# The first slab of a rotary-embedding kernel loaded by eight DMAs of every eighth partition

## The chip, the cores and the metric

The kernel runs on one core of a Trainium2 chip. The metric is the device time in microseconds (us), the median of repeated runs. Engines have the profile's names: ACT is the scalar engine, DVE the vector engine, SP the engine whose queue issues the loads.

## The reference

The input `x` is float32 of shape 16 x 512 x 1024 (batch, sequence, dimension), and the dimension is 16 heads of 64. Each head is rotated with a `cos` and a `sin` of its sequence position. The output is float32 of the same size.

```python
x = x.reshape(batch, seq, num_heads, head_dim)
x1, x2 = x[..., :half_dim], x[..., half_dim:]
rotated = np.concatenate([x1 * cos - x2 * sin, x1 * sin + x2 * cos], axis=-1)
```

So 33.55 MB come in and 33.55 MB go out, whatever the kernel does.

## The kernel before

The work is cut into 8 slabs of 2 batches each, 4 MB per slab. A slab lies in SBUF (the core's working memory of 128 partitions) as 128 rows of W = 8192 float32, 32 KB in each partition. One DMA loads it and one stores it. Five slab buffers are in turn; the first five loads are issued at once.

```python
    def dram(t, s, a=0, n=W):
        return bass.AP(tensor=t.tensor, offset=t.offset + s * nb * seq * dim + a,
                       ap=[[W, P], [1, n]])
    # ...
    def load(s):
        slab[s] = slabs.tile([P, W], f32, tag="slab", name="slab")
        nc.sync.dma_start(out=slab[s], in_=dram(x, s))

    load(0)
    # ... cos and sin are loaded with two small DMAs ...
    for s in range(1, slots):          # slots = 5
        load(s)
```

For each slab ACT casts to bf16, DVE multiplies twice and adds, ACT casts back to float32, and ACT's queue issues the store; then the slab's buffer is loaded again.

```python
        nc.scalar.copy(out=xs, in_=xu)
        if r + n == rpp:
            nc.scalar.dma_start(out=dram(out_flat, s), in_=slab[s])
            if s + slots < nslabs:
                load(s + slots)
```

Of the kernel before, what the change touches and what calls it, by code (L numbers as in the profile page):

```python
# [2 lines left out]

# [4 lines left out]


@with_exitstack  # L10
def kernel(
    ctx: ExitStack,
    tc: tile.TileContext,
    x: bass.AP,
    cos: bass.AP,
    sin: bass.AP,
    num_heads: int,
    out: bass.AP,
):
    nc = tc.nc  # L20
    P = nc.NUM_PARTITIONS

    batch, seq, dim = x.shape
    nh = num_heads
    hd = dim // nh
    half = hd // 2
    bf16 = mybir.dt.bfloat16
    f32 = mybir.dt.float32

    nb = 2  # L30
    slots = 5
    nslabs = batch // nb
    rpp = nb * seq // P
    W = rpp * dim
    SP = seq // rpp
    TW = rpp * half

    out_flat = out.rearrange("b s h d -> b s (h d)")

    singles = ctx.enter_context(tc.tile_pool(name="singles", bufs=1))  # L40
    slabs = ctx.enter_context(tc.tile_pool(name="slabs", bufs=slots))
    xpool = ctx.enter_context(tc.tile_pool(name="xpool", bufs=2))
    psum = ctx.enter_context(tc.tile_pool(
        name="psum", bufs=1, space=bass.MemoryType.PSUM))
# [7 lines that stand above are left out]
    def view(t, offset, *dims):  # L52
        return dataclasses.replace(t, offset=t.offset + offset,
                                   ap=[t.ap[0], *[list(d) for d in dims]])


    slab = {}


    def load(s):  # L60
        slab[s] = slabs.tile([P, W], f32, tag="slab", name="slab")
        nc.sync.dma_start(out=slab[s], in_=dram(x, s))  # L62


    load(0)


    TR = seq // P
    G = rpp // TR
    raw = singles.tile([P, 2 * TR * half], f32, tag="raw")  # L70
    for i, src in enumerate((cos, sin)):
        nc.gpsimd.dma_start(out=view(raw, i * TR * half, (1, TR * half)), in_=bass.AP(  # L72
            tensor=src.tensor, offset=src.offset,
            ap=[[TR * half, P], [1, TR * half]]))

    for s in range(1, slots):
        load(s)


    pick = singles.tile([P, G * P], bf16, tag="pick")  # L80
    nc.gpsimd.memset(pick, 0.0)  # L81
    for g in range(G):
        part = view(pick, g * P, (SP, P // SP), (1, SP))
        nc.gpsimd.affine_select(  # L84
            out=part, in_=part, compare_op=mybir.AluOpType.not_equal, fill=1.0,
            base=-g, pattern=[[0, P // SP], [-G, SP]], channel_multiplier=1)

    tab1 = singles.tile([P, 2 * TR * half], bf16, tag="tab1")
    nc.vector.tensor_copy(out=tab1, in_=raw)  # L89
    acc = psum.tile([P, 2 * TW], f32, tag="acc")  # L90
    for i in range(2):
        for g in range(G):
            nc.tensor.matmul(view(acc, i * TW + g * TR * half, (1, TR * half)),  # L93
                             view(pick, g * P, (1, P)),
                             view(tab1, i * TR * half, (1, TR * half)),
                             start=True, stop=True)

    tab = singles.tile([P, 2 * rpp * hd], bf16, tag="tab")
    nc.vector.tensor_copy(out=view(tab, 0, (hd, 2 * rpp), (1, half)),  # L99
                          in_=view(acc, 0, (half, 2 * rpp), (1, half)))  # L100
    nc.vector.tensor_copy(out=view(tab, half, (hd, rpp), (1, half)),  # L101
                          in_=view(acc, 0, (half, rpp), (1, half)))
    nc.vector.tensor_scalar_mul(  # L103
        out=view(tab, rpp * hd + half, (hd, rpp), (1, half)),
        in0=view(acc, TW, (half, rpp), (1, half)), scalar1=-1.0)

    xb = {}


    def cast(u):  # L110
        s, r, n = u
        if r == 0:
            xb[s] = xpool.tile([P, W], bf16, tag="xb", name="xb")
        nc.scalar.copy(out=view(xb[s], r * dim, (1, n * dim)),  # L114
                       in_=view(slab[s], r * dim, (1, n * dim)))



    passes = []
    for s in range(nslabs):  # L120
        n = rpp if s < nslabs - 2 else rpp // 2
        passes += [(s, r, n) for r in range(0, rpp, n)]


    cast(passes[0])
    for i, (s, r, n) in enumerate(passes):
        if i + 1 < len(passes):
            cast(passes[i + 1])
        xs = view(slab[s], r * dim, (1, n * dim))
        xu = view(xb[s], r * dim, (1, n * dim))  # L130

        t2 = view(slab[s].bitcast(bf16), 2 * r * dim, (1, n * dim))
        for t, a in ((t2, rpp * hd), (xu, 0)):
            nc.vector.tensor_mul(  # L134
                out=t, in0=xu,
                in1=view(tab, a + r * hd, (hd, n), (0, nh), (1, hd)))
        nc.vector.tensor_add(  # L137
            out=xu, in0=xu, in1=view(t2, half, (hd, n * nh), (-half, 2), (1, half)))
# [8 lines that stand above are left out]
# [1 line left out]
_INS = ['x', 'cos', 'sin', 'num_heads']  # L148
_OUTS = [((16, 512, 16, 64), 'float32')]

_NUMBERS = {'num_heads': 16}


# [26 lines left out]
```

## Time and profile before

| | before |
|---|---|
| time, median of 4 runs | 162.27 us (161.70 to 163.23) |
| span of the profiled run (that run took 163.08 us) | 161.3 us |
| DVE busy, ACT busy | 67%, 70% |
| DMA engine time: loads (q1), stores (q10) | 49.1%, 48.2% |
| first slab issued, landed | 0.74 us, 13.32 us |

The 16 DMA engines work 97.3% of the span, so this is a kernel bound by its transfers.

### The profile page before, as it was taken

The numbers are of one execution on the slowest core, as the hardware profiler recorded it, in microseconds if no ns is written. First come the engines' busy times: TensorE is split into PE (matmuls) and PEld (weight loads), VectorE is DVE, ScalarE is ACT, GpSimd is POOL, SyncE is SP. The second block draws the span as 40 slices with busy tenths as digits, with TensorE's granted clock in tenths as the row PEclk, the third lists the DMA queues.
The fourth block names the chain that finished last, engine by engine and source line by source line (L and its number), as shares of the span: only waits on it lengthen the run. The fifth ranks groups of instructions, "written<-read, shape, count | busy, mean of one in ns | idle before, by whom it ended". The sixth has DMA issues, their size and how long they took to land.

```text
span 161.3 us, 153 instructions
## 1 busy us (share of the span) xinstructions
PE 0.6 (0%) x4; PEld 0.4 (0%) x4; DVE 108.7 (67%) x34; ACT 113.5 (70%) x21; POOL 2.3 (1%) x9
## 2 busy tenths in 40 slices
PE   0010000000000000000000000000000000000000
PEld 0000000000000000000000000000000000000000
DVE  0012099999969997998899499939739399940000
ACT  3006939469899899989987997089994999653000
POOL 5000000000000000000000000000000000000000
DMA  7999999999989999999999999999999999999992
GB/s 260 406 406 390 520 390 390 520 390 390 488 349 463 390 439 471 390 439 471 382 447 455 398 447 455 398 447 455 390 439 463 398 431 471 398 431 471 398 431 106
DMA packets 2368, 67.24 MB, mean 417 GB/s; under 512 B 288, under 2 KB 288, under 8 KB 320
## 3 DMA queue, kind: packets, MB, share of 16 engines
q1 hardware_dynamic: 1152, 33.55, 49.1%
q10 hardware_dynamic: 1152, 33.55, 48.2%
q0 software_dynamic: 64, 0.13, 0.2%
HBM read 33.69 MB, written 33.55 MB: 417 GB/s over the span
## 4 chain that ended last, share of the span: by engine, by line
DMA 42%; ACT 33%; DVE 13%; issue 2%; ACTq 0%; SPq 0%
DMA slab<-in_x_dram 25%; DMA out_dram<-slab 18%; ACT slab L140 17%; ACT xb L114 16%; DVE slab L134 4%; DVE xb L134 4%; DVE xb L137 4%; ACTq L142 0%; ACTq L140 0%; SPq L62 0%
## 5 line engine op out<-in xcount | busy, mean ns | idle before, releaser
L114 ACT CAST xb<-slab 128x8192 bf16<-128x8192 f32 (+1 forms) x10 | 56.5, 5652 | 25.2 <-DMA slab<-in_x_dram 24.0
L140 ACT CAST slab<-xb 128x8192 f32<-128x8192 bf16 (+1 forms) x10 | 56.5, 5650 | 7.2 <-DVE xb L137 7.2
L134 DVE TENSOR_TENSOR slab<-xb,tab 128x8192 bf16<-128x8192 bf16 (+1 forms) x10 | 35.7, 3572 | 21.9 <-ACT xb L114 21.8
L137 DVE TENSOR_TENSOR xb<-xb,slab 128x8192 bf16<-128x8192 bf16 (+1 forms) x10 | 35.7, 3572 | 0.3
L134 DVE TENSOR_TENSOR xb<-xb,tab 128x8192 bf16<-128x8192 bf16 (+1 forms) x10 | 35.7, 3572 | 0.3
L89 DVE CAST tab<-raw 128x256 bf16<-128x256 f32 x1 | 0.3, 294 | 11.0 <-DMA raw<-in_sin_dram 11.0
L114 ACT ACT_TABLE_LOAD x1 | 1.3, 1283 | 0.7 <-PEq L161 0.7
L99 DVE CAST tab<-acc 128x512 bf16<-128x512 f32 x1 | 0.7, 691 | 0.7 <-PE acc L93 0.7
L72 POOL DMA_DIRECT2D raw<-in_cos_dram x1 | 0.7, 674 | 0.8 <-POOLq L161 0.8
L93 PE MATMUL acc<-tab,pick 128*128 128x128 bf16 x4 | 0.6, 302 | 11.3 <-DVE tab L89 11.3
L84 POOL TENSOR_SCALAR_AFFINE_SELECT pick<-pick 128x128 bf16<-128x128 bf16 x2 | 0.5, 288 | 0.1
L72 POOL DMA_DIRECT2D raw<-in_sin_dram x1 | 0.5, 534 | 0.0
L93 PEld LDWEIGHTS <-pick 128*128 128x128 bf16 x4 | 0.4, 127 | 11.2 <-issue 8.0
L101 DVE CAST tab<-acc 128x256 bf16<-128x256 f32 x1 | 0.4, 415 | 0.0
L103 DVE TENSOR_SCALAR tab<-acc 128x256 bf16<-128x256 f32 x1 | 0.4, 415 | 0.0
L81 POOL MEMSET pick<- 128x256 bf16 x1 | 0.3, 330 | 0.0
L161 POOL MEMSET const-float32-0.0<- 128x1 f32 x1 | 0.1, 99 | 0.2 <-issue 0.2
L161 POOL MEMSET const-bfloat16-1.0<- 128x1 bf16 x1 | 0.1, 102 | 0.0
L161 POOL MEMSET const-uint8-127<- 128x1 uint8 x1 | 0.1, 102 | 0.0
L161 POOL MEMSET const-float32-1.0<- 128x1 f32 x1 | 0.1, 99 | 0.0
## 6 DMA issues: line engine op xcount, KB each, us to landing
slab<-in_x_dram SPq DMA_DIRECT2D x8, 4096.0 KB, 27.3
out_dram<-slab ACTq DMA_DIRECT2D x8, 4096.0 KB, 24.0
raw<-in_cos_dram POOLq DMA_DIRECT2D x1, 64.0 KB, 7.0
raw<-in_sin_dram POOLq DMA_DIRECT2D x1, 64.0 KB, 9.0
```

What stands on the lines that cost most here:

```text
L72: nc.gpsimd.dma_start(out=view(raw, i * TR * half, (1, TR * half)), in_=bass.AP(tensor=src.tensor, offset=src.offset, ap=[[TR * half, P], ...
L81: nc.gpsimd.memset(pick, 0.0)
L84: nc.gpsimd.affine_select(out=part, in_=part, compare_op=mybir.AluOpType.not_equal, fill=1.0, base=-g, pattern=[[0, P // SP], [-G, SP]], c ...
L93: nc.tensor.matmul(view(acc, i * TW + g * TR * half, (1, TR * half)), view(pick, g * P, (1, P)), view(tab1, i * TR * half, (1, TR * half)) ...
L99: nc.vector.tensor_copy(out=view(tab, 0, (hd, 2 * rpp), (1, half)), in_=view(acc, 0, (half, 2 * rpp), (1, half)))
L101: nc.vector.tensor_copy(out=view(tab, half, (hd, rpp), (1, half)), in_=view(acc, 0, (half, rpp), (1, half)))
L103: nc.vector.tensor_scalar_mul(out=view(tab, rpp * hd + half, (hd, rpp), (1, half)), in0=view(acc, TW, (half, rpp), (1, half)), scalar1=-1.0)
L114: nc.scalar.copy(out=view(xb[s], r * dim, (1, n * dim)), in_=view(slab[s], r * dim, (1, n * dim)))
L134: nc.vector.tensor_mul(out=t, in0=xu, in1=view(tab, a + r * hd, (hd, n), (0, nh), (1, hd)))
L137: nc.vector.tensor_add(out=xu, in0=xu, in1=view(t2, half, (hd, n * nh), (-half, 2), (1, half)))
L140: nc.scalar.copy(out=xs, in_=xu)
L161: nc = _bacc.Bacc("TRN2", target_bir_lowering=False, num_devices=1)
```

## The change

Its intent is to give each of the 16 DMA engines one 32 KB row per DMA, eight times, instead of eight rows in one DMA. The bytes are the same.

```diff
-    load(0)
+    slab[0] = slabs.tile([P, W], f32, tag="slab", name="slab")
+    for p in range(P // 16):
+        nc.sync.dma_start(
+            out=slab[0][p::P // 16, :],
+            in_=bass.AP(tensor=x.tensor, offset=x.offset + p * W,
+                        ap=[[P // 16 * W, 16], [1, W]]))
```

## The prediction

The sum came to +9.0 us on 162.1 us, 171.1 us: +9.75 us for packets of the first slab that take twice the 1.22 us of the trace before, -0.4 us for sooner first bytes and another -0.3 us. The factor two and the -0.3 us stand as my estimates only. This slower case was given about 70%, with 169.5 to 173 us.

> **What bounds the kernel now.** I read the page first, its slices and its DMA queues. In the slices each digit is a fortieth of the span in tenths of busy time, and the row of GB/s is what the DMA engines moved.
>
> ```profile
> DMA  7999999999989999999999999999999999999992
> GB/s 260 406 406 390 520 390 390 520 390 390 488 349 463 390 439 471 390 439 471 382 447 455 398 447 455 398 447 455 390 439 463 398 431 471 398 431 471 398 431 106
> ...
> q1 hardware_dynamic: 1152, 33.55, 49.1%
> q10 hardware_dynamic: 1152, 33.55, 48.2%
> ...
> HBM read 33.69 MB, written 33.55 MB: 417 GB/s over the span
> ```
>
> The DMA row has a 9 (or one 8) from the second slice to the last but one: the 16 DMA engines are never out of work. Loads (q1) take 49.1% and stores (q10) 48.2% of all engine time, 97.3% together. No compute engine comes near: the page has DVE at 67% and ACT at 70%. From q1 I also get the unit that I need: 0.491 x 161.3 us x 16 engines = 1267 us for 8 loads x 128 rows of 32 KB = 1024 data packets, so 1.24 us for one 32 KB packet; q10 gives 1.22 us. That is 32,768 B / 1.22 us = 26.9 GB/s for one engine. A load of 4 MB is 8 such packets on each engine, 9.7 to 9.9 us.
>
> Next the chain that ended last, for its beginning and its longest pieces, and the list of waits.
>
> ```profile
> 0.74 12.58 DMA slab<-in_x_dram
> 13.32 0.02 issue
> 13.34 7.03 ACT xb L114
> ...
> 69.62 28.29 DMA out_dram<-slab
> 97.90 0.02 SPq L62
> 97.93 0.03 issue
> 97.96 27.38 DMA slab<-in_x_dram
> ```
> ```profile
> ACT xb L114 <- DMA slab<-in_x_dram: 24.0, 5, 11.3
> ```
>
> The chain starts with the very load that is changed: issued at 0.74 us, landed at 13.32 us. Of these 12.58 us some 9.8 are the packets and 2.8 are start and landing. ACT sits idle 11.3 us for it, and the first cast waits for the whole slab, not for pieces. The middle pieces look like compute and transfers in turn, but the slices say that the DMA engines are full through all of it, so the time is set by when they start, at which rate they run, and how long the tail is after them. Last the issuing queue and the end of the span:
>
> ```profile
> L62 SPq DMA_DIRECT2D slab<-in_x_dram x8: 328/398/600, 0.7 to 98.0; - x8
> ```
> ```profile
> 0.74 2.49 SPq L62 DMA_DIRECT2D slab<-in_x_dram  x5
> ```
> ```profile
> 150.00:155.00 5.00, 0.00 (x0) 0.00 (x0) 0.00 (x0) 0.00 (x0) 0.00 (x0) 1.00 1.03 446
> 155.00:158.00 3.00, 0.00 (x0) 0.00 (x0) 0.00 (x0) 0.00 (x0) 0.00 (x0) 1.00 0.96 415
> 158.00:161.30 3.30, 0.00 (x0) 0.00 (x0) 0.00 (x0) 0.00 (x0) 0.00 (x0) 1.00 0.07 30
> ```
>
> The first is the load's line (min/median/max ns of an issue), the second the timeline: all five first loads are issued in 2.49 us, without waits between them. The third is the busy table by stretch, whose last two columns are DMA share and GB/s: the engines run at full rate until about 158 us, then there is the landing of the last store.
>
> [...]
>
> **The change part by part.**
>
> *Bytes and packets: nothing.* 8 DMAs x 16 rows are the same 128 packets of 32 KB, 8 per engine[...]. The other 15 transfers of 4 MB stay.
>
> *Issues: added, but hidden.* SP gets 8 issues in place of 1. At the 0.33 to 0.60 us of the load's line they cost 2.6 to 4.8 us at the very most, and a DMA of 16 rows should be no dearer to issue than one of 128. An engine has 1.22 us or more of work from each, so it isn't starved; loads 1 to 4 are issued some 3 us later, when the engines are still busy with slab 0. Cost 0. The first issue now makes 16 rows instead of 128, so the first bytes may flow a little sooner: I take -0.4 us, a guess bounded by the 2.8 us of start and landing.
>
> *[...] this is where I expect the cost.* DMA number p writes partitions p, p+8, ... p+120[...] a packet takes 2 x 1.22 = 2.44 us and the slab 8 x 2.44 = 19.5 us in place of 9.75: +9.75 us. [...] I take -0.3 us. Compute is no part of it.
>
> *Who pays.* [...] no store exists yet (the first is issued at 40.88 us), so nothing fills the half-used engines. Slab 0 lands at 13.3 + 9.0 = 22.3 us, slab 1 some 10 us later, all stores later by the same, and the engines are full from then on as before. The lost time of the bound is not made good: +9.75 - 0.4 - 0.3 = **+9.0 us**, and 162.1 + 9.0 = **171.1 us**.
>
> *Waits.* [...] Some 0.1 us, in the rounding.
>
> **The rivals.**
>
> A. *The engines bind[...].* Then each engine has the same 8 packets at 1.22 us and nothing else changes; the earlier first byte gives up to 0.5 us: 161.6 to 162.3 us, the same. [...]
>
> B. *The eight DMAs wait for each other*, because their targets lie interleaved in one buffer, or because semaphores are used again. Each would cost start and landing, 2.8 + 1.2 = 4.0 us, eight of them 32 us in place of 12.6: +19 us, 181 us. Against it: the rows are disjoint, and the timeline has no wait between the loads of before. A milder form, in which only loads 1 to 4 wait for single pieces, costs nothing, as these are issued long before their turn.
>
> C. [...] the loss is smaller, 3 to 7 us, 165 to 169 us. [...]
>
> D. *The loss is hidden later.* It would need idle DMA time to be eaten up. The slices have none between the second and the last but one, so I give this next to nothing.
>
> **Range and chances.** [...] C another 8%, B 4%, and A 18%. A lies within 2% (158.9 to 165.3 us), nearly all the rest above. Faster by 2% would need over 3 us; the whole start and landing of slab 0 is 2.8 us, so almost nothing. Range 165.5 to 173.5 us, which leaves out A and B. Chances: faster 0.01, same 0.19, slower 0.80.
>
> **What would show it.** If right: the first piece of the chain grows from 12.58 to some 21.6 us; ACT's longest wait for the load from 11.3 to about 20; in a table by stretch the GB/s from 4 to 20 us lie near 215 while the DMA share stays near 1 (packets are longer, not fewer); the share of q1 stays near 49% or rises, as 128 packets cost 1.22 us more each (156 us of engine time: 1267 + 156 = 1423 us over 16 x 170.3 us is 52%); from 25 us on, the slices look as before, and the tail is the same. Wrong: if the stretch from 4 to 12 us shows some 420 GB/s, A holds; if it has gaps in the DMA share with waits of SP between issues of the first slab, B; if GB/s begin low and climb within the slab, C. If slab 0 lands late but the end doesn't move, D.

## The result

The changed kernel takes 172.06 us (171.81 to 172.16, 4 runs) against 162.27 us: slower, with a ratio of 1.0595 (95% interval 1.0541 to 1.0648). A ratio here is the mean time of one kernel's runs over that of the other's in the same rounds, so it isn't quite the ratio of the medians quoted beside it.

The page of the changed kernel, first its slices and the load queue:

```profile
DMA  5989979999999999999999898989898989898985
GB/s 133 268 185 193 239 285 455 409 455 409 455 409 455 409 455 432 432 439 424 463 401 478 385 486 378 486 378 486 378 486 378 486 378 486 378 493 378 486 378 239
...
q1 hardware_dynamic: 1264, 33.56, 52.0%
```

The DMA row is as full as before, but for the first six slices, some 25 us, the engines move only 133 to 285 GB/s. They are as busy as before and work at about half the speed. The load queue takes 52.0% of 16 x 170.0 us, 1414 us, where before it took 1267 us for the same bytes.

The busy table by stretch says it more exactly. Its columns are PE, PE weight load, DVE, ACT and POOL busy us, the clock, then DMA share and GB/s. A packet counts in the stretch in which it starts, so a share can be a little over 1. Before:

```profile
4.00:12.00 8.00, 0.59 (x4) 0.32 (x3) 0.35 (x2) 0.00 (x0) 0.00 (x0) 1.00 0.97 418
12.00:20.00 8.00, 0.00 (x0) 0.00 (x0) 1.30 (x3) 6.66 (x1) 0.00 (x0) 1.00 1.01 434
20.00:28.00 8.00, 0.00 (x0) 0.00 (x0) 7.57 (x2) 5.31 (x2) 0.00 (x0) 1.00 0.97 418
...
15.00:155.00 140.00, 0.00 (x0) 0.00 (x0) 107.06 (x30) 110.52 (x20) 0.00 (x0) 1.00 1.01 431
```

and after, each with a long stretch of its steady part added:

```profile
4.00:12.00 8.00, 0.58 (x4) 0.31 (x3) 1.65 (x4) 0.00 (x0) 0.00 (x0) 1.00 1.04 217
12.00:20.00 8.00, 0.00 (x0) 0.00 (x0) 0.00 (x0) 0.00 (x0) 0.00 (x0) 1.00 1.00 209
20.00:28.00 8.00, 0.00 (x0) 0.00 (x0) 0.00 (x0) 4.03 (x2) 0.00 (x0) 1.00 0.99 348
...
26.00:162.00 136.00, 0.00 (x0) 0.00 (x0) 107.06 (x30) 111.43 (x20) 0.00 (x0) 1.00 1.00 432
```

From 4 to 20 us the rate is 217 and 209 GB/s where it was 418 and 434. From 26 us on it is 432 GB/s, the old rate (431). Nothing is lost after the first slab, and nothing is won back.

The chain that ended last (followed back from the last instruction, each step to what released it), at its beginning, after:

```profile
0.74 0.57 SPq L68
...
5.23 18.64 DMA slab<-in_x_dram
...
23.96 1.28 ACT L120
```

The slab lands at 5.23 + 18.64 = 23.87 us, 10.55 us later than before. Two smaller things are new. The issue of one of the eight DMAs takes 0.57 us. And ACT loads its activation table (L120, 1.28 us) after the slab has landed; before, that was done at 0.74 us, while ACT waited. ACT now has four semaphore instructions at this line, from 16.6 to 23.9 us, and the table load stands behind those waits. Last come the wait of ACT and the waits of the issuing queue (total us, times, longest us), and the issues of the changed line (min/median/max ns):

```profile
ACT L120 <- DMA slab<-in_x_dram: 24.0, 1, 24.0
```
```profile
SPq L62 <- DMA slab<-in_x_dram: 14.4, 5, 4.8
```
```profile
L68 SPq DMA_DIRECT2D slab<-in_x_dram x8: 567/589/681, 0.7 to 5.2; - x8
```

The second shows that loads 1 to 4 now wait for landed pieces of slab 0 before they are issued: by the timeline they go out from 6.12 to 16.90 us, where before all five loads were out by 3.23 us. They still come in time: the DMA share is 1.04, 1.00 and 0.99 in the three stretches from 4 to 28 us.

For single packets I read the DMA packet records of the traces. The first number is the start of the first 32 KB packet of slab 0, in us from the start of the run's own span; then come the median durations (us) of its first 16 packets by start (taken as one per engine; the records kept don't name the engine), the next 16, and so on to the eighth. All kernels of this table but the first are explained in this document's experiments.

```
                          start   1st  2nd  3rd  4th  5th  6th  7th  8th
before                     1.76  1.93 1.22 1.21 1.21 1.21 1.22 1.22 1.21
after                      2.08  2.39 2.47 2.44 2.55 2.33 2.55 2.55 2.55
e2 sixteen neighbours      1.77  3.91 4.53 4.58 4.35 4.53 4.54 4.55 4.56
e4 every fourth            2.07  1.87 1.24 1.21 1.21 1.21 1.21 1.21 1.21
e5 halves in turn          2.09  2.25 2.39 2.23 2.31 2.31 2.31 2.31 2.31
e6 staggered, first trial  2.28  2.03 1.77 1.81 1.66 1.58 1.52 1.50 1.50
e9 staggered, second       2.11  2.25 1.67 1.55 1.40 1.46 1.34 1.42 1.42
e11 32 neighbours          1.78  2.29 2.56 2.55 2.54 2.51 2.58 2.55 2.56
```

(In e6 and e9 the eight packets of the added DMA shift the groups a little.) In the changed kernel a packet takes 2.55 us once the start is over, slightly more than twice 1.21 us.

### The profile page after: what moved, and what is told of

Same layout as the page of the kernel before. It is cut to its first block, busy times and chain, and to the rows that moved or that the text cites. A ratio compares the mean times of both kernels' runs of the same rounds, so it can differ in the third digit from the quotient of the medians.

```text
span 170.0 us, 169 instructions
## 1 busy us (share of the span) xinstructions
PE 0.6 (0%) x4; PEld 0.4 (0%) x4; DVE 108.7 (64%) x34; ACT 113.5 (67%) x21; POOL 2.3 (1%) x9
## 3 DMA queue, kind: packets, MB, share of 16 engines
q1 hardware_dynamic: 1264, 33.56, 52.0%
q10 hardware_dynamic: 1152, 33.55, 45.7%
HBM read 33.69 MB, written 33.55 MB: 395 GB/s over the span
## 4 chain that ended last, share of the span: by engine, by line
DMA 42%; ACT 33%; DVE 12%; SPq 2%; issue 2%; ACTq 0%
DMA slab<-in_x_dram 27%; ACT slab L146 17%; ACT xb L120 15%; DMA out_dram<-slab 15%; DVE xb L143 4%; DVE slab L140 4%; DVE xb L140 4%; SPq L68 2%; ACT L120 1%; ACTq L148 0%; ACTq L120 0%; ACTq L146 0%; SPq L62 0%
## 5 line engine op out<-in xcount | busy, mean ns | idle before, releaser
L120 ACT CAST xb<-slab 128x8192 bf16<-128x8192 f32 (+1 forms) x10 | 56.5, 5652 | 10.0 <-DMA slab<-in_x_dram 8.7
```

The costliest lines, as they stand in the source:

```text
L120: nc.scalar.copy(out=view(xb[s], r * dim, (1, n * dim)), in_=view(slab[s], r * dim, (1, n * dim)))
```

## The experiments

The theory to test is that the cost comes from which partitions are written at the same moment: in the change, 16 that lie eight apart. Why some sets of partitions should be slower than others is not shown by any run, and the mechanism that I had assumed is cut. The rivals to tell apart are the splitting itself (eight small DMAs, their issues and waits), DRAM rows 256 KB apart, and "a DMA's rate follows from the partitions that it writes as a whole" against "what counts is which partitions are written at the same moment". Every experiment was timed in 3 rounds beside the kernel before; the medians of that were 162.28 to 162.88 us.

| run | slab 0 (unless said) | time, us | ratio, 95% interval |
|---|---|---|---|
| e1 | 8 DMAs, 128 partitions, an eighth of the columns | 162.04 | 0.9959 (0.992 to 0.9997) |
| e2 | 8 DMAs of 16 neighbours | 188.38 | 1.158 (1.1537 to 1.1623) |
| e3 | as the change, DRAM rows in a row | 171.52 | 1.0549 (1.0502 to 1.0596) |
| e4 | 4 DMAs of every fourth partition | 162.94 | 1.0034 (0.9984 to 1.0085) |
| e5 | 8 DMAs, halves in turn | 170.45 | 1.0508 (1.0469 to 1.0548) |
| e6 | e5 and one 8-row DMA ahead | 168.61 | 1.0401 (1.0347 to 1.0454) |
| e7 | the last store split, load as before | 171.08 | 1.0558 (1.0487 to 1.063) |
| e8 | the change, table load early | 172.03 | 1.061 (1.0572 to 1.0648) |
| e9b | e5, upper half first | 170.84 | 1.0508 (1.0449 to 1.0566) |
| e9 | e9b and one 8-row DMA second | 166.19 | 1.0229 (1.0165 to 1.0292) |
| e10 | load 6 split, slab 0 as before | 174.62 | 1.0733 (1.0662 to 1.0803) |
| e11 | 4 DMAs of 32 neighbours | 171.99 | 1.0581 (1.0529 to 1.0633) |

The diffs below are shortened. Those of e1 to e5, e9b and e11 are against the change (with `P // 16` written as 8), that of e6 and e9 against its control, that of e8 against the change, those of e7 and e10 against the kernel before.

### e1: eight DMAs over all partitions

```diff
+    C = W // 8
     for p in range(8):
-        nc.sync.dma_start(out=slab[0][p::8, :], in_=...)
+        nc.sync.dma_start(out=view(slab[0], p * C, (1, C)), in_=dram(x, 0, p * C, C))
```

> Eight DMAs for the first slab, but each of all 128 partitions and an eighth of the columns (4 KB per row). [...] packets run at the full rate and the slab lands at about 13.5 to 14.5 us; time 162 to 164 us. Rival, the splitting into eight small DMAs costs the time by itself (their issues, their start and landing, their semaphores): landing near 24 us and about 172 us.

The line by stretch of e1:

```profile
4.00:12.00 8.00, 0.58 (x4) 0.31 (x3) 1.65 (x4) 0.00 (x0) 0.00 (x0) 1.00 1.03 411
```

411 GB/s and 162.04 us: eight issues and the waits that come with them cost nothing that can be seen here. The rival of the splitting falls. The ratio is below 1 by 0.4% with an interval that nearly touches 1; I take it as the same time.

### e2: the same DMAs with 16 neighbouring partitions

```diff
-            out=slab[0][p::8, :],
-            in_=bass.AP(tensor=x.tensor, offset=x.offset + p * W,
-                        ap=[[8 * W, 16], [1, W]]))
+            out=slab[0][16 * p:16 * p + 16, :],
+            in_=bass.AP(tensor=x.tensor, offset=x.offset + 16 * p * W,
+                        ap=[[W, 16], [1, W]]))
```

> Eight DMAs of 16 neighbouring partitions each, one 32 KB row per engine as in the change; only which partitions go together differs. [...] a packet takes four times 1.22 us, the slab 39 us in place of 19.5: landing near 43 us, 190 to 193 us. Rival, what costs is one-descriptor DMAs: about 172 us as with the change. Rival, the DRAM rows 256 KB apart: these are neighbours now, so about 162 us.

```profile
20.00:28.00 8.00, 0.00 (x0) 0.00 (x0) 0.83 (x3) 0.00 (x0) 0.00 (x0) 1.00 1.04 119
```

119 GB/s with the engines fully busy, packets of 4.5 us, 188.38 us. Against the change only the choice of partitions differs, and DRAM rows that are neighbours; against e3 below, which reads these very DRAM rows and took 171.52 us, nothing but the partitions differs. With 16 neighbours the packet takes 3.7 times the 1.21 us of before, with every eighth partition (2.55 us) 2.1 times. The four times of the expectation was an estimate of mine. The time is 1.6 us under the expected band; packets of 4.5 us in place of 4 x 1.22 = 4.88 us would account for it.

### e3: DRAM rows one after the other

```diff
-            in_=bass.AP(tensor=x.tensor, offset=x.offset + p * W,
-                        ap=[[8 * W, 16], [1, W]]))
+            in_=bass.AP(tensor=x.tensor, offset=x.offset + 16 * p * W,
+                        ap=[[W, 16], [1, W]]))
```

> As the change on the SBUF side (every eighth partition), but the 16 rows of each DMA lie one after the other in DRAM. The result is wrong on purpose: slab 0's rows are permuted. [...] nothing changes against the change, 171 to 173 us. Rival, DRAM rows 256 KB apart are read slowly: 162 to 163 us.

```profile
4.00:12.00 8.00, 0.58 (x4) 0.31 (x3) 0.36 (x2) 0.00 (x0) 0.00 (x0) 1.00 1.03 216
```

216 GB/s against 217: the distance of the rows in DRAM has no part in it. Its output is wrong, which doesn't matter for the time. The time is 0.5 us under the change's.

### e4: four DMAs of every fourth partition

```diff
-    for p in range(8):
+    for p in range(4):
         nc.sync.dma_start(
-            out=slab[0][p::8, :], ...            ap=[[8 * W, 16], [1, W]]))
+            out=slab[0][p::4, :], ...            ap=[[4 * W, 32], [1, W]]))
```

The first band is for a rate set by the partitions written at one moment, the second for one set by all the partitions of a DMA.

> Four DMAs of every fourth partition, 32 rows each, two per engine. [...] If what counts is[...] written at the same moment: 169.5 to 172 us, a little under the change[...]. If what counts is[...] a DMA reaches as a whole: 162 to 163 us.

```profile
4.00:12.00 8.00, 0.59 (x4) 0.32 (x3) 1.65 (x4) 0.00 (x0) 0.00 (x0) 1.00 1.07 459
```

Full rate, packets of 1.21 us, 162.94 us. My first band rested on an assumption of how the 32 rows are dealt to the engines, which no run shows. Either only the partitions of a whole DMA count, or the rows are dealt differently from what I assumed. The next runs had to decide whether the moment counts at all.

### e5, e9b: the controls

With 16 rows to a DMA it matters less how they are dealt: in the trace of the change, which has 16 rows to a DMA too, 16 packets are under way at each whole us from 3 to 23 us. Here they are every fourth partition of one half, the lower (0 to 63) or the upper (64 to 127).

```diff
-    for p in range(8):
-        nc.sync.dma_start(out=slab[0][p::8, :], ...)
+    for p in range(4):
+        for h in (0, 64):              # e9b: (64, 0)
+            nc.sync.dma_start(
+                out=slab[0][h + p:h + 64:4, :],
+                in_=bass.AP(tensor=x.tensor, offset=x.offset + (h + p) * W,
+                            ap=[[4 * W, 16], [1, W]]))
```

> Control for the next run. Eight DMAs of 16 rows, every fourth partition of one half: 0, 4, .. 60, then 64, 68, .. 124, then 1, 5, .. 61 and so on. [...] half rate as in the change[...]: 169.5 to 171.5 us. Rival, something particular to every eighth partition: 162 to 163 us.

> Control for the next run: the halves in turn, upper half first. Same as the halves in turn before, 170 to 171 us.

170.45 and 170.84 us, as expected; the line of e5:

```profile
4.00:12.00 8.00, 0.58 (x4) 0.31 (x3) 1.65 (x4) 0.00 (x0) 0.00 (x0) 1.00 1.08 241
```

Packets take 2.31 us against 2.55; in the change the fifth packet is the short one (2.33 us). Why these are shorter is not shown.

### e6, e9: the same DMAs, with half of the engines one packet behind

A DMA of 8 rows adds 8 packets under 512 B where each of the others adds 16 (q1 of e6 has 1280 packets: 1032 rows, 15 x 16 small packets of the other DMAs and 8 of this one), which I read as 8 engines in place of 16. Put into the queue, it is meant to make these one packet late for all that follows, so that with halves in turn some engines write to the lower half while the others write to the upper; the records don't name the engines, so this isn't seen directly. The added rows go into slab 1's buffer, which load 1 overwrites later (and waits for; the lines that allocate this buffer early and load it are left out of the diff). e6 has the added DMA first, on rows of the lower half, e9 second, on rows of the upper half, which the first DMA has written to. In both expectations the first band is for a full rate by staggering, the second for a cost that the moment has no part in.

```diff
+        if i == 0:                     # e9; in e6 ahead of the loop, rows 0:32:4
+            nc.sync.dma_start(
+                out=slab[1][64:96:4, :],
+                in_=bass.AP(tensor=x.tensor, offset=x.offset, ap=[[4 * W, 8], [1, W]]))
```

> The control with one more DMA ahead of it: 8 rows of 32 KB (into slab 1's buffer, which load 1 overwrites after)[...]. [...] full rate again in spite of more bytes, 162.5 to 165 us with about 1.2 us for the added packet. [...] 1.2 us above the control, 171 to 173 us.

> The staggering tried once more, with the added 8-row DMA second in the queue[...]. In the first trial (168.6 us) packets took about 1.5 us[...]. [...] first packet 2.4 us, then 1.22 to 1.4 us each, 165 to 167 us. [...] as the control and one packet, 171.5 to 172.5 us.

e6 took 168.61 us. That is over its band of 162.5 to 165, and still 1.8 us under its control although it moves more. Its packets of 1.50 to 1.81 us were still longer than 1.21 us, for a reason not shown, and I placed the added DMA differently. e9 took 166.19 us, inside its band, 4.7 us under its control e9b, with 256 KB more to move. The stretch from 4 to 12 us of e9, then of e9b:

```profile
4.00:12.00 8.00, 0.58 (x4) 0.32 (x3) 1.65 (x4) 0.00 (x0) 0.00 (x0) 1.00 1.01 344
...
4.00:12.00 8.00, 0.06 (x1) 0.05 (x1) 0.29 (x1) 0.00 (x0) 0.00 (x0) 1.00 1.03 225
```

Packets went from 2.36 us (e9b) to 1.34 to 1.67 us. The DMAs of slab 0 are the same ones, on the same partitions; only what is under way beside what has changed. So the rate isn't a property of a single DMA: at 344 GB/s against 225, it depends on what is written at the same moment. If that had no part in it, 171.5 to 172.5 us were expected. Two ends stay open. The packets are still above 1.21 us, and why isn't known; and no run staggers engines that stay on one half of the partitions, which would tell this apart from any other good that working on two DMAs at once may do.

### e11: four DMAs of 32 neighbouring partitions

What the run can show is whether 32 neighbours are as slow as the 16 of e2 (a quarter of the rate) or run like every eighth partition (half of it).

```diff
+    for p in range(4):
+        nc.sync.dma_start(
+            out=slab[0][32 * p:32 * p + 32, :],
+            in_=bass.AP(tensor=x.tensor, offset=x.offset + 32 * p * W,
+                        ap=[[W, 32], [1, W]]))
```

> Four DMAs of 32 neighbouring partitions, two rows per engine[...]. It asks how the rows of a DMA of 32 are dealt to the engines, which decides how every fourth partition (162.9 us) is to be understood. (a) [...] a quarter of the rate, 186 to 190 us. [...] (b) [...] half the rate, 170 to 172 us. (c) Only[...] that a DMA reaches as a whole count, whatever the dealing[...], half the rate, 170 to 172 us.

```profile
12.00:20.00 8.00, 0.59 (x4) 0.32 (x3) 1.01 (x3) 0.00 (x0) 0.00 (x0) 1.00 1.07 219
```

171.99 us, half the rate (190 GB/s from 4 to 12 us): (a), a quarter of the rate, is refuted as I had put it, (b) and (c), half of it, both fit. How 32 rows are dealt to the engines, and so how e4 is to be understood, is not shown. The practical reading doesn't need it: four DMAs over every fourth partition run at full rate (459 GB/s from 4 to 12 us, e4), four over neighbours at half.

### e7: the last store instead of the first load

```diff
-            nc.scalar.dma_start(out=dram(out_flat, s), in_=slab[s])
+            if s < nslabs - 1:
+                nc.scalar.dma_start(out=dram(out_flat, s), in_=slab[s])
+            else:
+                for p in range(8):
+                    nc.scalar.dma_start(
+                        out=bass.AP(tensor=out_flat.tensor, offset=out_flat.offset
+                                    + s * nb * seq * dim + p * W,
+                                    ap=[[8 * W, 16], [1, W]]),
+                        in_=slab[s][p::8, :])
```

> The kernel before, with its last store split as the change splits the first load: eight DMAs of every eighth partition out of SBUF. [...] the last slab takes 19.5 us in place of 9.7, some of it beside the store before it, 168 to 172 us. If only writes into SBUF meet this limit: 162 to 163 us.

```profile
150.00:155.00 5.00, 0.00 (x0) 0.00 (x0) 0.00 (x0) 0.00 (x0) 0.00 (x0) 1.00 1.13 243
155.00:160.00 5.00, 0.00 (x0) 0.00 (x0) 0.00 (x0) 0.00 (x0) 0.00 (x0) 1.00 0.96 249
```

243 and 249 GB/s at the end, where the kernel before had 446 from 150 to 155 us; 171.08 us. The engines are as busy as before (shares of 1.13 and 0.96), so this read from SBUF slows down much as the load did (217 and 209 GB/s). The step between the rows in DRAM, which e3 clears for loads, wasn't tested alone for a store.

### e8: the table load taken off the chain

```diff
+    warm = singles.tile([P, 1], f32, tag="warm")
+    nc.vector.memset(warm, 0.0)
+    nc.scalar.copy(out=warm, in_=warm)
```

> The change with a copy of one element on ACT at the start, so that the 1.28 us activation table load is done before the waits and not after them (in the changed kernel it moved from 0.7 us to 24 us, onto the chain). If the DMA engines set the end: stores start 1.3 us sooner and nothing comes of it, 171.5 to 172.5 us. If the chain's compute pieces are the bound: 1.3 us less, 170.5 to 171 us.

The table load was back at 0.74 us, and the issues of the stores, min/median/max ns and first and last start, show the first one at 51.6 us, where the changed kernel has 52.8:

```profile
L152 ACTq DMA_DIRECT2D out_dram<-slab x8: 338/338/374, 51.6 to 155.3; - x8
```

The time stayed at 172.03 us. 1.2 us sooner on the chain's compute bought nothing. This is also why the pieces "ACT" and "DVE" of the chain, nearly half of it by share, must not be read as a bound here.

### e10: load 6 split, in mid-kernel

```diff
     def load(s):
         slab[s] = slabs.tile([P, W], f32, tag="slab", name="slab")
-        nc.sync.dma_start(out=slab[s], in_=dram(x, s))
+        # s == 6: eight DMAs out=slab[s][p::8, :] as in the change; else as before
```

> The kernel before with load 6, in mid-kernel beside stores, split as the change splits the first load. If the loss is the same wherever there is a full DMA queue: about 9 us, 170 to 172 us. If the stores that share the engines fill the time[...]: clearly less, 163 to 168 us.

174.62 us, worse than either reading. Three lines of its table by stretch, the two queues of its page, and the issue of its eight DMAs in the timeline (start, us from the first to the end of the last):

```profile
90.00:100.00 10.00, 0.00 (x0) 0.00 (x0) 4.34 (x2) 10.00 (x2) 0.00 (x0) 1.00 1.03 331
140.00:150.00 10.00, 0.00 (x0) 0.00 (x0) 6.32 (x3) 10.00 (x3) 0.00 (x0) 1.00 0.83 357
150.00:160.00 10.00, 0.00 (x0) 0.00 (x0) 7.44 (x4) 6.54 (x3) 0.00 (x0) 1.00 0.73 315
```
```profile
q1 hardware_dynamic: 1264, 33.56, 49.0%
q10 hardware_dynamic: 1152, 33.55, 45.8%
```
```profile
78.18 22.11 SPq L64 DMA_DIRECT2D slab<-in_x_dram  x8
```

Beside stores, and with its pieces spread over a longer time, the rate falls less, to 331 GB/s rather than 217 and 209. But the eight issues took 22.11 us, as the queue waited between them for earlier transfers (its list of waits has 23.6 us on stores and 9.3 us on loads at that line), the slab came late for the compute, and towards the end the DMA engines ran dry: shares of 0.83 (140 to 150 us) and 0.73, where no 10 us stretch of the kernel before, from 30 to 150 us, is under 0.97. So there are both longer packets and idle engines in the 11.7 us, and the queues say how much is which: packets took 94.8% of 173.3 us, 164.3 us per engine, against 97.3% of 161.3 us, 156.9 us, before. That is 7.4 us of longer packets; the remaining 4.6 us of the 12.0 us by which the span grew are time without packets. That the waits between the issues made it idle is argued, not tested. Neither expectation had the waits.

## Why the prediction was right

It forecast 171.1 us (165.5 to 173.5) and 172.06 was measured. By its steps:

- *Bytes and packets, nothing.* Right: 1264 packets on q1 are the 1152 of before and 7 x 16 packets of 4 bytes, and the megabytes are the same (33.56 against 33.55).
- *Packets twice as long, +9.75 us.* Right that the choice of partitions costs it: e1, e2, e3, e5 and e9 single it out against the splitting, DRAM and the DMAs as such. The mechanism is not shown. In size: load time on q1 went from 1267 to 1414 us, which is 147 us over 16 engines, +9.2 us, where the prediction had 9.75 - 0.3 = 9.45. The two small tables take part (q0 from 0.2% to 0.4% of engine time, +0.35 us).
- *The -0.3 us.* About right in size: one packet of eight was shorter by 0.2 us (2.33 against 2.55 us). The reason for it no run shows.
- *First bytes, -0.4 us.* Wrong in sign. The first packet started at 2.08 us in place of 1.76, +0.3 us. The first issue took 0.57 us in place of 0.37 (medians of the line 0.59 and 0.40), where I had said that 16 rows should be no dearer than 128; as 16 neighbours took 0.42 us (e2) and every eighth partition 0.59 us with the same DRAM rows (e3), it is the step between the rows in SBUF that is dear, not their number. The 2.8 us that bounded the guess were misread, too: by the packet records before, 1.0 us pass from the first issue to the first packet and 0.5 us from the last packet to the landing; the rest lies among the packets, whose first took 1.93 us.
- *Issues hidden.* Right that they don't starve the engines: the DMA share was 1.04 and 1.00 while the slab came in. But loads 1 to 4 were issued 5 to 14 us later than before, by their waits, and not some 3 us later.
- *Who pays.* Right: 432 GB/s from 26 to 162 us against 431 from 15 to 155 us before, so the loss stays. By the packet records the last one ends at 168.7 us against 160.1, which is 8.6 us, as the span grew by 8.7 us. That is less than the 9.8 us of the medians because the profiled run of before was one of its slower ones (163.08 us) and that of after its fastest (171.81): before, three last packets ended late, at 159.2, 160.0 and 160.1 us, the others by 158.9. The mean end of the last 16 packets of 4 bytes in the store queue is 168.4 us against 158.8, 9.7 us.
- *Waits, 0.1 us.* Here it overlooked that the table load goes behind the waits: 1.28 us on the chain. e8 shows that this was worth nothing in time.

The measured terms, 9.2 + 0.35 + 0.3 us, make 9.9 us, and the time grew by 9.8 us. The forecast sum was 9.05 us: the start explains some 0.7 of the 0.8 us that it lacked. A little luck is in the rest, as the tables' 0.35 us, which it didn't have, and the 0.25 us that it had too much for the packets nearly cancel.

Of its signs, the 215 GB/s (217 and 209) and the share of q1 (52%) came as forecast. The landing was 23.9 us in place of 22.3, about half of it by the start (+0.3 us where -0.4 was forecast) and about half by packets of up to 2.55 in place of 2.44 us. ACT's longest wait was 24.0 us rather than 20, since without the table load ahead of it ACT waits from the start.

Of the rivals, A (the engines bind) fell with the result. B in its milder form was real: loads 1 to 4 waited for pieces, and it cost nothing here, as said; in e10 there were such waits, and idle engines after them. C, a loss of 3 to 7 us only, didn't happen by itself; e9, staggered on purpose, lost 3.3 us. D fell.

## What to carry to other kernels

Before splitting a DMA by partitions, write down which partitions are written at each moment, not only how many rows, bytes and engines there are: equal packets, with the DMA share near 1, still ran at half rate on every eighth partition (217 and 209 GB/s) and at about a quarter on 16 neighbours (119 GB/s), where the kernel before had 418 and 434. If such a transfer has to be split, split it by columns over all 128 partitions, or by every fourth partition: here these ran at 411 and 459 GB/s. In this kernel, which is bound by its transfers, the loss was paid at the first load (9.8 us) and at the last store (8.6 us) alike, while 1.3 us of compute on the "chain that ended last" was worth nothing.
